# A DeltaNet inverse whose levels mask only the columns they fill, in six shared tiles per layer

## The chip, the core and the metric

One NeuronCore of a Trainium2 chip runs the whole program. The metric is the time of one execution on the device in microseconds. Engines are named as the profile names them: PE multiplies matrices (PEld is its weight load), DVE is the vector engine, ACT the scalar engine, POOL the general one, SP only issues transfers. Each engine runs its own instructions in the order in which the program lists them.

## The reference, cut to what matters

The kernel computes a two-layer backbone: three token mixers side by side (differential attention, grouped-query attention, a gated DeltaNet in both directions), merged by gates, then a feed-forward part. The change touches the DeltaNet, where each chunk needs the inverse of a unit triangular matrix:

```python
kb = kc * bc[..., None]
a_low = jnp.where(strict, jnp.einsum('bhncd,bhnsd->bhncs', kb, kc) * decay, 0.0)
eye = jnp.eye(DN_CHUNK, dtype=jnp.float32)
tmat = lax.linalg.triangular_solve(a_low + eye, jnp.broadcast_to(eye, a_low.shape),
                                   left_side=True, lower=True, unit_diagonal=True)
u = tmat @ (vc * bc[..., None])
w = tmat @ (kb * jnp.exp(gcum)[..., None])
...
def step(s, inp):
    u_i, w_i, kt_i, gl_i = inp[:4]
    v_new = u_i - jnp.einsum('bhcd,bhde->bhce', w_i, s)
    s_next = s * gl_i[..., None, None] + jnp.einsum('bhcd,bhce->bhde', kt_i, v_new)
```

## The kernel before, in words

Activations lie with features on the partitions; 512 latent and 256 context tokens make 768 columns. **Dense projections** are matmuls of a weight block `wl` with the activations `hh`, `hl` (float32 is split into a high and a low part, so each product is three matmuls) into PSUM banks `pf`; the four weight buffers are filled by a load `wr` and split by ACT and by DVE or POOL (`wunit`, L493).

**The DeltaNet** uses chunks of 128 tokens. `dn_prep` (L1435) prepares one chunk step of a pair of heads in both directions: four 128x128 matrices side by side, 512 columns, called A below. It needs one slot, the tile `pres` (its thirds hold A, its 16-bit copy and the half tile `ym`, and the decay), and one third of the shared tile `dnw` for `u16` and `t16`, the running inverse and its transpose. After a first level it runs levels 1 to 6 (L1497): PE forms `py` = A times `u16` (4 matmuls of 128 columns, 16 bit), DVE masks `py` with `lev` into `ym` (all 512 columns, though half of each matrix is only the identity), PE forms `pt` = `ym` times `t16` (4 matmuls of 128 columns) and `pu` (4 of 64 columns, the new columns alone), ACT copies `pt` into `t16` and DVE copies `pu` into the new columns of `u16` (`new_cols`, L1427). Then come two correction rounds: each is a product, a subtraction from the identity on DVE, a product and an addition on DVE, the second round in float32; POOL makes the 16-bit remainder of A before and scales the result by `beta` after (4 instructions each step). Twelve preps per layer run, two at a time. `dn_pair` (L1544) carries the state through the six steps of a head pair in sequence: product with the state, `rp` on DVE (4 instructions), product, copy on ACT, product, new state on DVE (4 instructions), and two products for the output, which DVE adds into `oacc`; it gives back four slots only at its end (`drop(4)`, L1605). It runs first for heads 0 and 1, then for heads 2 and 3.

**What sets the order.** A planner in the kernel (`Est`, L75, and `Sched`, L175) keeps an estimate of each engine's time and writes the instructions of all these chains into one program: at each point it takes a chain whose operands are estimated to be ready, by priority, and else one more matmul of the current dense job. So PE's order is fixed when the program is built, and the dense matmuls are what stands between the steps of a DeltaNet chain. The estimate of a DVE instruction grows with its columns.

**Slots.** All larger tiles come from one pool of `NSLOT` = 15 slots (L41). A chain or job that asks for slots says so first, "w" or "W" for each, and `room` (L249) grants a "W" only if `reserve` slots stay free besides:

```python
n = need.count("w") + need.count("W") + need.count("V")
spare = self.reserve if "W" in need else 1 if "V" in need else 0
return (n + spare <= self.left["w"] and all(need.count(c) <= self.left[c] for c in "tr")
        and all(need.count(c) <= len(self.est.idle[c]) for c in "mb" if c in need))
```

While the attention runs, `reserve` is 3; once only the DeltaNet is left it is 2 (L1865). The remaining DeltaNet inputs are dense jobs: `dn_inputs` (L1337) projects one head's q, k and v, asks for "tWW" before the first of the three (L1345: one tile `qk`, one tile `kv`), and the jobs stand in a line. A gate projection may stand in for a waiting job only where `reserve` is 3 (L325). The modulation products (`wm` with `cond`, `mod_late`, L572) also ask for "WW".

Of the kernel before, what the change touches and what calls it, by code (L numbers as in the profile page):

```python
# [13 lines left out]
F16 = mybir.dt.float16  # L14
BF16 = mybir.dt.bfloat16
AF = mybir.ActivationFunctionType
ALU = mybir.AluOpType
# [3 lines left out]
P = 128  # L21
# [17 lines left out]
NLEV = 7  # L39
# [339 lines left out]
def trunk(  # L379
# [5 lines left out]
    out, dbg=None,  # L385
# [3 lines left out]
    V, S, G, T = [Timed(e, k, est, tc) for e, k in ((nc.vector, "V"), (nc.scalar, "S"), (nc.gpsimd, "G"), (nc.tensor, "P"))]  # L389
# [5 lines left out]
    const = ctx.enter_context(tc.tile_pool(name="const", bufs=1))  # L395
# [31 lines left out]
    def slot(parts, n, nm, dt=F32):  # L427
        t = whole(parts, n, nm, dt)
        return [t[:, i, :] for i in range(parts)]
# [5 lines left out]
    def drop(n=1):  # L435

        sch.left["w"] += n
# [14 lines left out]
    def psml():  # L452
        return est.take("m", pools["m"].tile([P, 512], F32, tag="pm", name="pm"))

    def give(*banks):

        for t in banks:
            est.give("m", t)

    sch = Sched(est, lambda src, n: wunit(src, n))  # L460
# [10 lines left out]
    ident16 = const.tile([P, P], F16, name="ident16")  # L471
# [4 lines left out]
    nc.sync.dma_start(out=sel, in_=sel_d)  # L476
    m12 = const.tile([P, 2, 2, P], BF16, name="m12")
    nc.gpsimd.dma_start(out=m12, in_=m12_d)
    lev = const.tile([P, NLEV, 2, P], BF16, name="lev")
    nc.gpsimd.dma_start(out=lev, in_=lev_d)  # L480
    ones = const.tile([P, 1], F32, name="ones")
    V.memset(ones, 1.0)
    mhalf = const.tile([P, 24], F32, name="mhalf")
# [9 lines left out]
    def wunit(src, n):  # L493

        while sch.left["r"] < 1:
            sch.flush([g for g in sch.groups if g[4]][:1])
        sch.left["r"] -= 1
        hl = wl_.tile([P, 2, 1024], F32R, tag="wl", name="wl")
        raw = wr_.tile([P, 1024], F32, tag="wr", name="wr")
        nc.sync.dma_start(out=raw[:, 0:n], in_=src)  # L500
        lo_n[0] += 1
        eng = "G" if lo_n[0] % lo_n[1] == 0 else "V"

        def halves():
            for a, b in ((0, n // 2), (n // 2, n)):
                yield "S"
                S.copy(out=hl[:, 0, a:b], in_=raw[:, a:b])
                yield eng
                (G if eng == "G" else V).tensor_tensor(out=hl[:, 1, a:b], in0=raw[:, a:b], in1=f32(hl[:, 0, a:b]), op=ALU.subtract)
            sch.left["r"] += 1  # L510
        g = sch.defer(halves())
        g[4] = True
        return hl, g
# [9 lines left out]
    cond = const.tile([P, KC, 2 * MOD_N + 30], F32, name="cond")  # L523
# [896 lines left out]
    def v4(t):  # L1420
        return t.rearrange("p (d i c) -> p d i c", d=2, i=2)
# [5 lines left out]
    def new_cols(t, b):  # L1427


        base = t.rearrange("p (d n c) -> p d n c", d=2, c=b)  # L1430
        n = 2 * P // (2 * b)
        st = list(base.ap)
        return bass.AP(base.tensor, base.offset + b, [list(st[0]), [2 * P - b, 2], [2 * b, n], [1, b]])

    def dn_prep(l, hp, s, heads, gates, nq, work, res):  # L1435

        beta, g, gc, ngc, egc, negc, gl, kts = gates
        un = units(hp, s)
        heads = [heads[hp * 2 + i] for i in range(2)]
        a32, uc, qd = slot(3, 512, "pres")  # L1440
        if l == 0:
            for d in range(2):
                r = (FWD, BWD)[d][s] * 8 + d * 4 + hp * 2
                nc.sync.dma_start(out=a32[:, d * 256:(d + 1) * 256].rearrange("p (i c) -> p i c", i=2),
                                  in_=gr[r:r + 2].rearrange("(o i) c -> o i c", o=1).to_broadcast([P, 2, P]))
        e1 = work()
        a16, ym = [uc.bitcast(F16)[:, i * 512:(i + 1) * 512] for i in range(2)]
        u16, t16 = [e1.bitcast(F16)[:, i * 512:(i + 1) * 512] for i in range(2)]
# [33 lines left out]
        py = psml()  # L1482
        for sl, *_ in un:
            T.matmul(py[:, sl], lhsT=a16[:, sl], rhs=ident16, start=True, stop=True)
        V.tensor_tensor(out=v4(u16), in0=v4(py), in1=lev[:, 0].unsqueeze(2).to_broadcast([P, 2, 2, P]), op=ALU.mult)
        give(py)
        for d in range(2):
            V.tensor_tensor(out=v4(t16)[:, d], in0=v4(a16)[:, d], in1=lev[:, 0, 1 - d].unsqueeze(1).to_broadcast([P, 2, P]), op=ALU.mult)
        if any(t < nq for _, _, _, t, _ in un):
            yield "m"  # L1490
            pq = psml()
# [4 lines left out]
        yield "m"  # L1496
        for lv in range(1, NLEV):  # L1497
            b = 1 << lv
            py = psml()
            for sl, *_ in un:  # L1500
                T.matmul(py[:, sl], lhsT=a16[:, sl], rhs=u16[:, sl], start=True, stop=True)
            V.tensor_tensor(out=v4(ym), in0=v4(py), in1=lev[:, lv].unsqueeze(2).to_broadcast([P, 2, 2, P]), op=ALU.mult)
            give(py)
            yield "mm"
            pt = psml()
            for sl, *_ in un:
                T.matmul(pt[:, sl], lhsT=ym[:, sl], rhs=t16[:, sl], start=True, stop=True)
            pu = psml()
            for u, (sl, i, d, t, c) in enumerate(un):
                new = ym[:, sl].rearrange("p (n e c) -> p n e c", e=2, c=b)[:, :, 1 - d, :]  # L1510
                T.matmul(pu[:, u * 64:(u + 1) * 64].rearrange("p (n c) -> p n c", c=b), lhsT=t16[:, sl], rhs=new, start=True, stop=True)
            S.copy(out=t16, in_=pt)
            V.tensor_copy(out=new_cols(u16, b), in_=pu[:, 0:256].rearrange("p (d n c) -> p d n c", d=2, c=b))
            give(pt, pu)
            if lv < NLEV - 1:
                yield "m"

        G.tensor_tensor(out=ym.bitcast(BF16), in0=a32, in1=a16, op=ALU.subtract)
        for it in range(2):
            yield "m"  # L1520
            py = psml()
            for sl, *_ in un:
# [3 lines left out]
                else:  # L1526
# [3 lines left out]
                            in1=py.rearrange("p (u c) -> p u c", u=4), op=ALU.subtract)  # L1530
            give(py)
            yield "m"
            py = psml()
# [178 lines left out]
    def chunks8(nt, nm):  # L1712
        r = []
        for _ in range(4):
            r += slot(2, nt, nm)
        return r
# [18 lines left out]
    for l in range(DEPTH):  # L1735
# [3 lines left out]
        nq = nt // P  # L1739
# [51 lines left out]
        vs, res, kts, vgs, gres, hres, gates = {}, {}, [], [], {}, {}, []  # L1791
# [40 lines left out]
            sch.spawn(mod_chain(MOD_A, MOD_ROOM[0], MOD_PACE[0]), 3)  # L1832


        prep, oacc, zs, dsteps, ws0, alone = {}, {}, {}, {0: 0, 1: 0}, [], []

        def work(n):
            if not ws0:
                ws0.extend(slot(3, 512, "dnw"))
            return ws0[n % 2]  # L1840

        def preps():
            for n in range(2 * NTC):
                hp, s = divmod(n, NTC)

                def cond(n=n, hp=hp):
                    return (sum(dsteps.values()) >= n - 2 and hp * 2 + 1 in hres and hp * 2 in hres and len(gates) > 0
                            and (len(alone) > 0 or len(done) >= PREP_AT and sch.left["w"] >= PREP_LEFT))
                yield cond, dn_prep(l, hp, s, hres, gates, nq, lambda n=n: work(n), prep), "w" if n else "ww"

        def pairs():
            yield lambda: (0, 0) in prep and (len(alone) > 0 or len(done) >= PAIR_AT)
# [21 lines left out]
        i = 1 if l == 0 else 2  # L1874
        sch.spawn(mod_chain((MOD_D, MOD_F)[l], MOD_ROOM[i], MOD_PACE[i]), 3)
        sch.run()
        drop(2)
        lo_n[1] = 3
        assert sch.left == {"w": NSLOT, "t": 2, "r": 2}, sch.left
        sch.left["w"] = 1 << 30  # L1880
# [5 lines left out]
        m = chunks8(nt, "m")  # L1886
# [111 lines left out]
def _consts():  # L1998
    pos = np.arange(LAT)
    inv = (10000.0 ** (-np.arange(0, 32, 2, dtype=np.float32) / np.float32(32))).astype(np.float32)  # L2000
    ar = (pos // 64).astype(np.float32)[:, None] * inv[None]
    ac = (pos % 64).astype(np.float32)[:, None] * inv[None]
    c = np.concatenate([np.cos(ar), np.cos(ac)], 1)
    s = np.concatenate([np.sin(ar), np.sin(ac)], 1)
    rope = np.stack([np.concatenate([c, c], 1), np.concatenate([s, -s], 1)], 0)
    rope = rope.reshape(2, LAT // P, P, HD).transpose(0, 2, 1, 3)
    i = np.arange(P)
    le = (i[:, None] <= i[None, :]).astype(np.float32)
    half = (i < P // 2).astype(np.float32)[:, None]
    up = np.stack([le, le.T], 1)  # L2010
    mid = np.stack([le - half, le.T - (1 - half)], 1)
    tri = np.stack([up, mid, 1 - up], 1)
    lt = i[None, :] < i[:, None]
    strict = np.stack([lt, lt.T], 1)
    m1 = np.where(strict, -BIG, BIG)
    incl = np.stack([i[:, None] <= i[None, :], i[:, None] >= i[None, :]], 1)
    m2 = np.where(incl, BIG, -BIG)
    m12 = np.stack([m1, m2], 1).astype(np.float32)
    lev = np.zeros((P, NLEV, 2, P), np.float32)
    for n in range(NLEV):  # L2020
        b = 1 << n
        same = (i[:, None] // (2 * b)) == (i[None, :] // (2 * b))
        first = (i // b) % 2 == 0
        mk = same & first[:, None] & ~first[None, :]
        lev[:, n, 0] = np.eye(P) - mk
        lev[:, n, 1] = np.eye(P) - mk.T
    sel = np.tile(np.eye(32), (4, 1))
    return [np.ascontiguousarray(a, np.float32) for a in (rope, np.eye(P), tri, sel, m12, lev)]

# [61 lines left out]
```

## Time and profile before

| | |
|---|---|
| median of 3 runs | 2910.73 us (2908.31 to 2911.45) |
| profiled execution | 2909.93 us |
| its span, first to last instruction | 2908.2 us |
| granted TensorE clock, mean | 0.994 |
| PE busy | 2835.2 us, 97% |
| DVE busy | 1699.2 us, 58% |
| ACT busy | 1226.8 us, 42% |
| POOL busy | 811.3 us, 28% |

The profiled execution lies 0.8 us below the median; 1.7 us of it lie outside the span. The DeltaNet of the first layer lies between about 565 and 900 us of the span, that of the second between about 2090 and 2425 us. In a row of the profile, x and a number is how many instructions it stands for; line L167 is a helper that records every operation, so rows are told apart by tile names. The matmuls' ends are modelled: a burst of matmuls is shown until its last result has left the array.

### The profile page before, as it was taken

The page shows a single profiled execution, that of the slowest core. Times are in us where ns is not written, and L with a number is a line of the kernel's source. Part 1 is how long each engine was busy: PE and PEld are TensorE (multiplying, and loading weights), DVE is VectorE, ACT ScalarE, POOL GpSimd, SP SyncE. Part 2 cuts the span into 40 slices and gives each one's busy share as a digit, 9 for nine tenths or more (in the row PEclk, how much of TensorE's full clock was granted, in tenths as well). Part 3 has the DMA queues.
Part 4 walks back from the last instruction along what each step waited for, and adds up shares of the span by engine and source line. Part 5 has one row for each costly group of instructions (what it writes and reads, how often), then busy time and mean ns, then how long its engine had stood idle before and what let it go on. Part 6 is the DMA issues. An engine that isn't in the chain of part 4 may idle for free.

```text
span 2908.2 us, 48877 instructions
## 1 busy us (share of the span) xinstructions
PE 2835.2 (97%) x19304; PEld 2460.5 (85%) x19304; DVE 1699.2 (58%) x3433; ACT 1226.8 (42%) x2522; POOL 811.3 (28%) x832
## 2 busy tenths in 40 slices
PE   7999999999999999999999999999999999999999
PEld 5888898888788888888888889898878788888888
DVE  4555767868766545333334456577787866553343
ACT  4444556645443224222222345466654443343332
POOL 3414231123322432112112242441123333422221
PEclk9999999999999999999999999999999999999999
DMA  8242211241312631121212321212131316323332
GB/s 312 90 147 77 68 49 55 62 157 59 113 57 97 221 109 59 51 73 53 72 58 68 97 75 55 61 59 62 57 122 44 132 66 203 127 85 107 97 98 87
DMA packets 100117, 271.99 MB, mean 94 GB/s; under 512 B 14209, under 2 KB 26417, under 8 KB 99889
## 3 DMA queue, kind: packets, MB, share of 16 engines
q1 hardware_dynamic: 88800, 247.31, 26.5%
q10 hardware_dynamic: 10800, 20.98, 1.8%
q8 instruction: 152, 2.49, 0.4%
q0 software_dynamic: 288, 0.59, 0.1%
q14 instruction: 77, 0.62, 0.1%
HBM read 240.56 MB, written 28.86 MB: 93 GB/s over the span
## 4 chain that ended last, share of the span: by engine, by line
PE 56%; DVE 3%; POOL 2%; issue 1%; ACT 1%; DMA 1%; SPq 0%; POOLq 0%; ACTq 0%; DVEq 0%
PE pf L167 46%; PE pm L167 7%; PE pb L167 2%; DVE wl L167 0%; POOL wl L167 0%; POOL m L167 0%; POOL pres L167 0%; DVE mx L167 0%; DMA th<-gd 0%; DVE dnw L167 0%; DVE oacc L167 0%; DVE pres L167 0%; POOL rn L167 0%; POOL rtmp L167 0%; DVE p L167 0%
## 5 line engine op out<-in xcount | busy, mean ns | idle before, releaser
L167 PE MATMUL pf<-hh,wl 128*128 128x512 f32 (+1 forms) x4192 | 1022.6, 359 | 9.9 <-ACT hh L167 6.2
L167 PEld LDWEIGHTS pf<-hh,wl 128*128 128x128 f32 x4192 | 698.1, 190 | 105.0 <-ACT hh L167 9.2
L167 POOL TENSOR_TENSOR wl<-wr,wl 128x512 fp32r<-128x512 f32 (+3 forms) x258 | 326.0, 1280 | 940.0 <-ACT wl L167 934.1
L167 PE MATMUL pf<-hl,wl 128*128 128x512 f32 (+1 forms) x2096 | 575.7, 359 | 0.9 <-POOL hl L167 0.6
L167 ACT CAST wl<-wr 128x512 fp32r<-128x512 f32 (+3 forms) x620 | 341.2, 588 | 491.0 <-PE pf L167 423.4
L167 PEld LDWEIGHTS pf<-hl,wl 128*128 128x128 f32 x2096 | 361.0, 190 | 47.6 <-POOL hl L167 1.8
L167 PE MATMUL pf<-wl,hh 128*128 128x256 f32 (+2 forms) x1664 | 321.7, 288 | 0.0
L167 PE MATMUL pf<-g,wl 128*128 128x512 f32 (+1 forms) x1629 | 307.3, 350 | 0.0
L167 PEld LDWEIGHTS pf<-g,wl 128*128 128x128 f32 x1629 | 263.8, 189 | 42.3 <-ACT g L167 1.9
L167 DVE TENSOR_TENSOR wl<-wr,wl 128x512 fp32r<-128x512 f32 (+4 forms) x362 | 263.3, 751 | 51.5 <-ACT wl L167 49.7
L167 PEld LDWEIGHTS pf<-wl,hh 128*128 128x128 f32 x1664 | 264.5, 192 | 5.9 <-issue 4.1
L167 PE MATMUL pf<-wl,hl 128*128 128x256 f32 (+2 forms) x832 | 241.1, 290 | 0.0
L167 DVE SCALAR_TENSOR_TENSOR x<-pf,gate,x 128x512 f32<-128x512 f32 (+1 forms) x126 | 80.4, 640 | 243.6 <-PE pf L167 237.0
L167 PE MATMUL pm<-dnw,pres 128*128 128x128 f16 (+1 forms) x1824 | 195.3, 236 | 6.2 <-POOL pres L167 3.0
L167 DVE SCALAR_TENSOR_TENSOR ff<-pf,cf,ff 128x511 f32<-128x511 f32 (+1 forms) x132 | 86.9, 658 | 184.5 <-ACT ff L167 183.2
L167 ACT ACTIVATE p<-pb,nb,r 128x768 f32<-128x768 f32 (+1 forms) x160 | 145.1, 908 | 104.5 <-DVE nb L167 82.7
L167 PE MATMUL pf<-ohl,wl 128*128 128x512 f32 (+1 forms) x864 | 171.6, 359 | 1.5 <-DVE ohl L167 0.7
L167 PEld LDWEIGHTS pf<-ohl,wl 128*128 128x128 f32 x864 | 143.9, 191 | 26.4 <-DVE ohl L167 1.8
L167 PEld LDWEIGHTS pf<-wl,hl 128*128 128x128 f32 x832 | 160.1, 192 | 2.7 <-issue 2.5
L167 DVE TENSOR_REDUCE mx<-pb 128x1 f32<-128x768 f32 (+1 forms) x160 | 133.5, 845 | 41.1 <-PE pb L167 39.9
L167 ACT CAST dnw<-pm 128x512 f16<-128x512 f32 x144 | 83.9, 585 | 143.8 <-PE pm L167 140.3
L167 PEld LDWEIGHTS <-pres 128*128 128x128 f16 (+1 forms) x1440 | 87.3, 98 | 58.2 <-issue 32.3
(246 smaller groups left out, 4083.9 us busy)
## 6 DMA issues: line engine op xcount, KB each, us to landing
wm<-in_w_mod_dram SPq DMA_DIRECT2D x96, 512.0 KB, 5.4
wr<-in_w_dram SPq DMA_DIRECT2D x88, 512.0 KB, 3.6
wr<-in_w_f_dram SPq DMA_DIRECT2D x80, 512.0 KB, 3.6
wr<-in_w_t_dram SPq DMA_DIRECT2D x32, 512.0 KB, 3.7
wr<-in_w_br_dram SPq DMA_DIRECT2D x24, 512.0 KB, 3.6
wr<-in_w_dram SPq DMA_DIRECT2D x32, 384.0 KB, 3.1
wr<-in_w_dram SPq DMA_DIRECT2D x32, 320.0 KB, 2.9
gd<-th ACTq DMA_DIRECT2D x24, 384.0 KB, 2.3
```

Source lines behind the costliest of these rows:

```text
L167: ins = f(*args, **kw)
```

## The change

A level masks only the 256 columns that it fills. The product `ym` moves out of the prep's own slot into six tiles, one per level, that all preps of a layer share: one slot `dny`, taken by the first prep. POOL writes the identity into each of the six once per layer; a level then writes its new columns over it and nothing else. So that two preps don't use one level's tile at once, a prep asks before each level whether its tile is in use. The first prep of a layer asks for three slots in place of two, and the layer gives back three at the end. The masks `lev` are laid out anew on the host; their size in memory is the same.

```diff
-    def dn_prep(l, hp, s, heads, gates, nq, work, res):
+    def dn_prep(l, hp, s, heads, gates, nq, work, yms, res):
...
         for lv in range(1, NLEV):
             b = 1 << lv
+            yield lambda lv=lv: lv not in yms()[-1] and sch.room("m")
+            yms()[-1].add(lv)
             py = psml()
             for sl, *_ in un:
                 T.matmul(py[:, sl], lhsT=a16[:, sl], rhs=u16[:, sl], start=True, stop=True)
-            V.tensor_tensor(out=v4(ym), in0=v4(py), in1=lev[:, lv].unsqueeze(2).to_broadcast([P, 2, 2, P]), op=ALU.mult)
+
+            yl = yms()[lv - 1]
+            V.tensor_tensor(out=new_cols(yl, b), in0=new_cols(py, b), in1=levn[lv].rearrange("p (d n c) -> p d n c", d=2, c=b), op=ALU.mult)
             give(py)
             yield "mm"
             pt = psml()
             for sl, *_ in un:
-                T.matmul(pt[:, sl], lhsT=ym[:, sl], rhs=t16[:, sl], start=True, stop=True)
+                T.matmul(pt[:, sl], lhsT=yl[:, sl], rhs=t16[:, sl], start=True, stop=True)
             pu = psml()
             for u, (sl, i, d, t, c) in enumerate(un):
-                new = ym[:, sl].rearrange("p (n e c) -> p n e c", e=2, c=b)[:, :, 1 - d, :]
+                new = yl[:, sl].rearrange("p (n e c) -> p n e c", e=2, c=b)[:, :, 1 - d, :]
                 T.matmul(pu[:, u * 64:(u + 1) * 64].rearrange("p (n c) -> p n c", c=b), lhsT=t16[:, sl], rhs=new, start=True, stop=True)
+            yms()[-1].remove(lv)
...
+        def yms():
+            if not ys:
+                t = whole(3, 512, "dny").bitcast(F16)
+                ys.extend(t[:, i // 2, i % 2 * 512:(i % 2 + 1) * 512] for i in range(NLEV - 1))
+                ys.append(set())
+                for y in ys[:NLEV - 1]:
+                    G.tensor_copy(out=y.rearrange("p (u c) -> p u c", u=4), in_=ident16.unsqueeze(1).to_broadcast([P, 4, P]))
+            return ys
...
-                yield cond, dn_prep(l, hp, s, hres, gates, nq, lambda n=n: work(n), prep), "w" if n else "ww"
+                yield cond, dn_prep(l, hp, s, hres, gates, nq, lambda n=n: work(n), yms, prep), "w" if n else "www"
...
-        drop(2)
+        drop(3)
```

The change moves instructions on every engine, since the planner's estimate of a mask falls with its columns and one slot less is free. Three places follow. In them `pf` are dense matmuls, `wm` modulation products; a product of a level reads `pres` (A, and before the change `ym`) or `dny` (the new tiles) and `dnw`; LDWEIGHTS is the weight load of the 16-bit matmul behind it; each such pair stands four times.

PE, first layer, levels of the fifth and sixth prep, the last two of heads 0 and 1, before:

```order
L167 MATMUL pm<-dnw,pres 128x128
L167 LDWEIGHTS dnw
L167 MATMUL pm<-pres,dnw 128x64
...
L167 MATMUL pf<-hh,wl 128x256 x2
L167 MATMUL pf<-hl,wl 128x256 x2
L167 MATMUL pf<-hh,wl 128x256 x2
...
L167 MATMUL pm<-identr,kv 128x128 x4
```

In the program before, dense matmuls or transposes of the next head's inputs stand between the products of one level and the next; the longest piece of PE's order in the two DeltaNet stages without a dense or modulation matmul has 59 rows.

PE, first layer, the same preps and the step of `dn_pair` behind them, with the change:

```order
L167 MATMUL pf<-hh,wl 128x512
L167 LDWEIGHTS pres
L167 MATMUL pm<-dnw,pres 128x128
...
L167 LDWEIGHTS dny
L167 MATMUL pm<-dnw,dny 128x128
...
L167 MATMUL pm<-dny,dnw 128x64
...
L167 MATMUL pm<-dnw,qk 128x128 x4
L167 MATMUL pm<-dnw,pres 128x128
L167 MATMUL pm<-wm,cond 32x256
```

Between that `pf` row and that `wm` row stand 286 rows, all of the DeltaNet: the last four levels of two preps in step and half of one before, both preps' corrections, and one and a half steps of `dn_pair`. In the second layer there is one such piece of 260 rows; no other piece of either stage has more than 58.

POOL, first layer, the first prep, with the change:

```order
L167 TENSOR_TENSOR wl<-wr,wl 128x512 x2
L167 TENSOR_TENSOR pres<-pres 128x512
L167 COPY dny<-ident_88 128x512 x6
L167 TENSOR_TENSOR wl<-wr,wl 128x512 x4
L167 TENSOR_SCALAR pres<-pres,beta 128x128 x8
```

The six copies are new; they stand behind two remainders of A and ahead of the low halves of four weight blocks' pieces.

## Rows read from the trace of the kernel before

**Rows 1.** The page, part 1: busy us (share of the span), instructions.

```profile
PE 2835.2 (97%) x19304; PEld 2460.5 (85%) x19304; DVE 1699.2 (58%) x3433; ACT 1226.8 (42%) x2522; POOL 811.3 (28%) x832
```

**Rows 2.** Both DeltaNet stages: length, busy PE, PEld, DVE, ACT, POOL, clock, DMA share, GB/s.

```profile
560.00:945.00 385.00, 379.00 (x3300) 325.20 (x3299) 282.57 (x636) 177.77 (x398) 113.30 (x114) 1.00 0.29 97
2080.00:2430.00 350.00, 342.50 (x2933) 280.13 (x2932) 265.19 (x594) 167.90 (x365) 111.64 (x118) 1.00 0.28 93
```

**Rows 3.** PE's waits, first layer's stage, 560 to 945 us: total, times, longest.

```profile
PE pm L167 <- DVE pres L167: 2.0, 3, 1.6
PE pm L167 <- POOL pres L167: 1.3, 3, 0.7
...
PE pm L167 <- DVE dnw L167: 0.7, 3, 0.3
```

**Rows 4.** PE's waits, second layer's stage, 2080 to 2480 us.

```profile
PE pm L167 <- DVE oacc L167: 2.7, 2, 1.8
PE pm L167 <- DVE dnw L167: 2.1, 3, 1.8
PE pm L167 <- POOL pres L167: 1.9, 2, 1.2
```

**Rows 5.** DVE's groups by shape: busy us, mean ns | idle before, releaser.

```profile
L167 DVE TENSOR_TENSOR pres<-pm,lev 128x512 f16<-128x512 f32 x144 | 97.4, 686 | 31.3 <-PE pm L167 29.8
...
L167 DVE CAST dnw<-pm 128x256 f16<-128x256 f32 x144 | 59.9, 420 | 28.1 <-PE pm L167 27.0
...
L167 DVE SCALAR_TENSOR_TENSOR dnw<-pm,negc,kv 128x128 f32<-128x128 f32 x80 | 22.5, 342 | 6.8 <-PE pm L167 6.7
...
L167 DVE TENSOR_TENSOR otmp<-pm,otmp 64x256 f32<-64x256 f32 x40 | 16.8, 420 | 12.7 <-ACT otmp L167 12.0
...
L167 DVE TENSOR_TENSOR pres<-identr,pm 128x512 bf16<-128x512 f32 x24 | 16.3, 682 | 10.0 <-PE pm L167 10.0
...
L167 DVE TENSOR_TENSOR oacc<-pm,oacc 128x128 f32<-128x128 f32 x40 | 9.7, 281 | 6.9 <-PE pm L167 6.8
```

**Rows 6.** ACT's and POOL's groups by shape.

```profile
L167 ACT CAST dnw<-pm 128x512 f16<-128x512 f32 x144 | 83.9, 585 | 143.8 <-PE pm L167 140.3 <-DVE gate L167 1.2 <-ACT kv L167 0.2
...
L167 POOL TENSOR_TENSOR wl<-wr,wl 128x512 fp32r<-128x512 f32 x214 | 284.5, 1345 | 794.8 <-ACT wl L167 788.9 <-DVE pres L167 5.8
L167 POOL TENSOR_SCALAR pres<-pres,beta 128x128 f32<-128x128 f32 x96 | 62.2, 666 | 102.8 <-DVE pres L167 95.5 <-DVE modF L167 7.3
...
L167 POOL TENSOR_TENSOR pres<-pres 128x512 bf16<-128x512 f32 x24 | 28.6, 1195 | 75.7 <-PE pm L167 70.1 <-DVE pres L167 5.5
```

**Rows 7.** Timeline, first layer, one level of two preps: start us, us, engine, operation.

```profile
603.43 0.40 PE L167 MATMUL pm<-dnw,pres 128*128 128x128 f16 x4
...
603.66 0.28 PE L167 MATMUL pm<-pres,dnw 128*128 128x64 f16 x4
...
603.78 0.39 PE L167 MATMUL pm<-dnw,pres 128*128 128x128 f16 x4
...
603.98 0.77 DVE L167 CAST dnw<-pm 128x256 f16<-128x256 f32 x2 [0.93 <-PE pm L167]
...
604.46 0.38 PE L167 MATMUL pm<-dnw,pres 128*128 128x128 f16 x4
...
604.88 1.29 DVE L167 TENSOR_TENSOR pres<-pm,lev 128x512 f16<-128x512 f32 x2
...
605.73 0.40 PE L167 MATMUL pm<-dnw,pres 128*128 128x128 f16 x4
```

**Rows 8.** Timeline near 706.85 us: four float32 products of the DeltaNet (eight matmuls).

```profile
706.85 1.06 PE L167 MATMUL pm<-dnw,pres 128*128 128x128 f32 x8
```

**Rows 9.** Stretches at the end of the second stage, columns as in rows 2.

```profile
2423.00:2427.00 4.00, 2.19 (x11) 1.36 (x10) 3.19 (x5) 0.93 (x2) 4.00 (x4) 1.00 0.01 4
2427.00:2431.00 4.00, 3.10 (x10) 2.62 (x11) 2.50 (x4) 0.00 (x0) 0.30 (x1) 0.50 0.61 197
2431.00:2435.00 4.00, 4.00 (x13) 3.18 (x12) 0.45 (x1) 0.00 (x0) 0.00 (x0) 0.64 1.00 322
```

More of the change, by code (lines that the diff above doesn't have):

```diff
@@ L478, in trunk @@
     nc.gpsimd.dma_start(out=m12, in_=m12_d)
-    lev = const.tile([P, NLEV, 2, P], BF16, name="lev")
+    lev = const.tile([P, 2 * NLEV, P], BF16, name="lev")
     nc.gpsimd.dma_start(out=lev, in_=lev_d)
+    lev0, levn = lev[:, 0:2], [lev[:, 2 * n:2 * n + 2].rearrange("p a c -> p (a c)") for n in range(NLEV)]
     ones = const.tile([P, 1], F32, name="ones")
@@ L1484, in dn_prep @@
             T.matmul(py[:, sl], lhsT=a16[:, sl], rhs=ident16, start=True, stop=True)
-        V.tensor_tensor(out=v4(u16), in0=v4(py), in1=lev[:, 0].unsqueeze(2).to_broadcast([P, 2, 2, P]), op=ALU.mult)
+        V.tensor_tensor(out=v4(u16), in0=v4(py), in1=lev0.unsqueeze(2).to_broadcast([P, 2, 2, P]), op=ALU.mult)
         give(py)
         for d in range(2):
-            V.tensor_tensor(out=v4(t16)[:, d], in0=v4(a16)[:, d], in1=lev[:, 0, 1 - d].unsqueeze(1).to_broadcast([P, 2, P]), op=ALU.mult)
+            V.tensor_tensor(out=v4(t16)[:, d], in0=v4(a16)[:, d], in1=lev0[:, 1 - d].unsqueeze(1).to_broadcast([P, 2, P]), op=ALU.mult)
         if any(t < nq for _, _, _, t, _ in un):
@@ L1832, in trunk @@
             sch.spawn(mod_chain(MOD_A, MOD_ROOM[0], MOD_PACE[0]), 3)
-        prep, oacc, zs, dsteps, ws0, alone = {}, {}, {}, {0: 0, 1: 0}, [], []
+        prep, oacc, zs, dsteps, ws0, alone, ys = {}, {}, {}, {0: 0, 1: 0}, [], [], []
         def work(n):
@@ L2024, in _consts @@
         mk = same & first[:, None] & ~first[None, :]
-        lev[:, n, 0] = np.eye(P) - mk
-        lev[:, n, 1] = np.eye(P) - mk.T
+        for d, m in enumerate((mk, mk.T)):
+            if n == 0:
+                lev[:, n, d] = np.eye(P) - m
+            else:
+                new = ~first if d == 0 else first
+                lev[:, n, d] = np.concatenate([(np.eye(P) - m)[:, new]] * 2, 1)
+    lev = lev.reshape(P, 2 * NLEV, P)
     sel = np.tile(np.eye(32), (4, 1))
```

## The prediction

> **What bounds the kernel now.** I read the page's busy times first, then the two DeltaNet stages as stretches, then PE's waits inside them. PE is busy for 97% of the span [rows 1]; no other engine comes near. The time is therefore PE's work plus PE's idle time, and a step on DVE counts only where PE waits for it. In the two stages, 385 and 350 us long, PE is idle for 6.0 and 7.5 us [rows 2]. The waits that belong to the DeltaNet's preparation are 2.0, 1.3 and 0.7 us in the first [rows 3] and 2.1 and 1.9 us in the second, where another 2.7 us are the tail of its output, `oacc` [rows 4]. So the chain of a prep, long as it is, is covered almost everywhere by dense matmuls that the planner puts between its steps. All that a shorter mask can win is these 8.0 us; everything else depends on the cover staying.
>
> **What the change removes.** 144 masks of 512 columns at 686 ns become masks of 256. DVE's product out of PSUM with 256 float32 results takes 420 ns, and its copy into the same strided columns also takes 420, so strides cost nothing there [rows 5]. I take 0.42 us: 0.27 us less per mask, 38 us of DVE in all. DVE is busy for 58% [rows 1], so this is worth nothing by itself. Per prep the chain gets six times 0.27 us shorter. POOL's remainder of A, 1.195 us [rows 6], no longer has to wait until the last level has read `ym`; it can be done earlier. Both take from the 8.0 us of waits; those on masks and on POOL are about half of them, so I take 4 us back, between 0 and 8.
>
> **What it adds.** PE's work is the same, matmul for matmul. POOL writes 512 columns of identity twelve times. The trace has no such copy: two-source work of that width takes 1.345 us, a one-source 128 columns 0.666 us [rows 6], so 0.6 to 1.4 us each, 4 to 8 us in a row per layer. POOL is busy for 28% [rows 1]. Behind them on POOL stand the low halves of weights and the scaling of the first preps; the planner splits weight blocks up to four ahead of their use, and PE would have to run through those first, so I cost the copies at nothing. If that cover were gone the whole row would be paid, up to 8 us per layer. The first level needs only the first copy. The wait for a tile in use is nothing either: the planner holds the second prep back until PE's two products are written down, and PE runs them in order anyway.
>
> **The slot is what costs.** After the attention, slots are held by `qk` and `kv` of three heads (6), `dnw` (2), `oacc` (1) and two or three `pres`: 11 or 12 of 15. Head 3's inputs ask for two with two in reserve, so they need 4 free. Before, there are 4 whenever only two `pres` live. With `dny` there are 3 at most, so the job stands until `dn_pair` of heads 0 and 1 ends and gives four back. The dense line stands behind it, no gate projection may take its place with a reserve of 2, and the modulation products ask for the same four. PE's order shows the outcome: one piece of 286 rows in the first layer and one of 260 in the second hold nothing but DeltaNet, where 59 was the most before.
>
> What do these pieces cost? First the levels. Two preps go in step. By the timeline [rows 7] four products of 128 columns take 0.23 us of PE before the next burst starts, four of 64 take 0.12, so PE's work for one level of both is 2 x (0.23 + 0.12 + 0.23) = 1.16 us. The chain of one prep is: `pt` 0.23, `pu` until its last result 0.28, to DVE 0.04, copy 0.42, back to PE 0.09, `py` 0.38, to DVE 0.04, mask 0.42, back 0.17: 2.07 us (it was 2.34). The second prep's DVE steps fit between, since DVE has 4 x 0.42 = 1.68 us. So each level without dense work leaves PE 0.91 us idle. The first layer has four such levels and one half covered: 4.1 us. The second has three: 2.7 us.
>
> Then the corrections and the state. Four float32 products take about 1.0 us [rows 8], 16-bit ones 0.40 with their drain [rows 7]. The first prep's corrections are 0.62 (eight matmuls) + 0.68 + 0.40 + 0.68 + 1.06 + 0.68 + 0.40 + 0.68 and 0.67 of hand-overs (four of 0.04, three of 0.17): 5.9 us. The second prep, one level and part of a correction behind on the same DVE, ends at about 10.0 us. In the first layer DVE then makes `rp` (4 x 0.342 [rows 5]); the product with it starts at 10.5 and ends at 11.9; ACT copies for 0.585 [rows 6]; the state's product starts at 12.7, its four DVE steps end at 14.6; the output's sums, 4 x (0.281 + 0.342), at 17.1; the next `rp` lets the next product start at about 18 us. PE's own work up to there is ten 16-bit bursts, one of 64 columns, and eight float32 products: 10 x 0.23 + 0.12 + 8 x 0.97 = 10.2 us. PE loses about 8 us. In the second layer the second prep lies a level further behind and fills some of the gaps; the same count gives 6 us up to the next `wm`, and 1 us when the second prep's result is scaled on POOL after it: 7 us.
>
> Bounds: if the estimate's order is loose and DVE or ACT still work off a dense job there, each piece loses up to 4 us more; if the two preps and the state run fully side by side, the second part loses half, 4 and 3.5 us.
>
> **The clock.** In 2423 to 2427 us PE was busy for 2.19 of 4 us, and for the next 8 us the granted clock was 0.50 and 0.64, half of 2.4 GHz for most of it [rows 9]: 3.4 us of full clock lost. The new pieces are thin too, 1.16 us of work in 2.07. I take one fall per layer, half of it hidden since PE waits there anyway: 2 x 1.7 = 3.4 us; bounds 0 and two whole falls per layer, 13.6. The Trainium skill ("TensorE: Matmul & The Clock Gate", Part 1) says that the low clock is the default state and that activity releases it. By that rule the falls would last as long as the thin pieces do. The trace agrees that it returns once PE is full again: 1.00 from 2435 us on.
>
> **Sum.** 4.1 + 8 + 2.7 + 7 - 4 + 3.4 = 21.2 us on the profiled execution's 2909.93 us, which lies 0.8 us below the median: **2931 us**, 0.7% slower. A measurement of this kernel can tell about 0.2%, 5.8 us, from no change.
>
> **Rivals.**
> 1. *The shorter chain wins* (faster). If the pieces' idle time is only moved, because preps that run ahead let later stages, the `oacc` tail with its 2.7 us and its clock fall among them, run without waits, 8.0 + 2.7 + 3.4 = 14.1 us come back; with 7 us left as the price of both pieces that is 2903 us. It decides if the two pieces together lose less than 14.1 us. For it: in the first layer the change has 10 us of gate projections behind the last DeltaNet product. Against: PE's total work is fixed, and an idle microsecond in a piece isn't given back by fuller stretches elsewhere. Chance 0.07.
> 2. *The pieces are thin, but cost little*: half the loss of the second parts, no clock fall, 8 us regained: 21.8 / 2 - 8 = 3 us, 2913 us. For it: chains on four engines overlap better than my hand count. Chance 0.13.
> 3. *The clock stays low through the pieces* and what follows: 13.6 in place of 3.4, 2941 us. For it: rows 9. The page named above would have it so for as long as PE stays thin. Chance 0.2.
> 4. *The change doesn't do what it says*: the strided mask takes as long as before (0.68 us), levels then take 2.34 us, and 7 more levels' 0.27 us are lost: 2933 us. Inside the range; chance 0.03, and 0.57 for the forecast itself.
>
> **How the numbers follow.** Forecast, rival 3 and rival 4 are slower by over 0.2%, as is a small part of rival 2: 0.83. Faster is rival 1 with some of its span within the bound: 0.06. The rest, 0.11, is no difference. The range leaves out rival 1 and the lower half of rival 2 below, and the worst of rival 3 above: 2913 to 2945 us.
>
> **What would show it.** Right: masks of 256 columns at 0.42 us; two stretches of about 25 us, around 690 and 2240 us of the span, with PE idle for 10 to 13 us each, waiting for DVE and POOL on `dny`, `pres` and `dnw`, and no `pf` in them; a clock of 0.5 in or right behind them. Wrong: PE's waits in the two stages together below 13 us, or a new wait on POOL's copies at the first prep. If the stretches are there but cost 5 us each, the hand-overs are what I mis-sized; if they cost 20, it is the clock.

## The result, and the profile after

With the change the kernel takes 2927.53 us (median of 4 runs, 2925.80 to 2929.83) beside 2909.95 us for the kernel before (4 runs, 2908.31 to 2911.45): ratio 1.0057, 95% interval 1.0045 to 1.0069. It is slower by 17.6 us, three times the 5.8 us that a measurement tells from no change; the forecast was 21.2 us slower. The profiled execution took 2926.18 us, 16.25 more than that of before.

The page of the changed kernel, part 1 (columns as in [rows 1]):

```profile
PE 2838.1 (97%) x19304; PEld 2465.7 (84%) x19304; DVE 1676.0 (57%) x3433; ACT 1225.2 (42%) x2522; POOL 817.3 (28%) x844
```

Beside [rows 1] PE's work is the same, matmul for matmul, though its busy time reads 2.9 us more; DVE has 23.2 us less to do, POOL 12 instructions and 6.0 us more. So at least 13 of the 16 us are idle time of PE. Where it lies shows in both DeltaNet stages, the changed kernel first, then the kernel before over the same stretches (columns as in [rows 2]):

```profile
560.00:955.00 395.00, 381.57 (x3301) 325.34 (x3301) 273.57 (x644) 176.70 (x398) 116.24 (x121) 1.00 0.28 95
2090.00:2450.00 360.00, 346.71 (x2951) 287.75 (x2951) 257.10 (x597) 168.49 (x366) 115.35 (x124) 1.00 0.28 93
```

```profile
560.00:955.00 395.00, 389.00 (x3359) 333.86 (x3358) 289.91 (x648) 179.02 (x400) 113.30 (x114) 1.00 0.30 100
2090.00:2450.00 360.00, 352.50 (x2946) 287.42 (x2945) 268.60 (x599) 166.97 (x364) 112.17 (x119) 0.99 0.31 103
```

PE is idle for 13.4 and 13.3 us where it was idle for 6.0 and 7.5. The second figure of a row understates the loss, since the modelled ends of short bursts count as busy. PE's waits in the changed kernel, first layer (560 to 955 us), then second (2090 to 2490 us), as in [rows 3, 4]:

```profile
PE pm L167 <- DVE dnw L167: 4.2, 6, 1.5
PE pm L167 <- DVE pres L167: 2.1, 5, 0.8
PE pm L167 <- DVE dny L167: 2.0, 3, 1.2
...
PE pm L167 <- DVE dnw L167: 6.5, 9, 1.7
PE pm L167 <- DVE oacc L167: 1.5, 1, 1.5
PE pm L167 <- DVE dny L167: 1.3, 3, 0.6
```

The waits on POOL's `pres`, 1.3 and 1.9 us before, are gone; those on `dnw`, 0.7 and 2.1 us, have grown to 4.2 and 6.5. The new time lies in one place per layer. PE in the first layer, from the last dense matmul before the piece to the first product of the modulation behind it:

```profile
712.79 0.47 PE L167 MATMUL pf<-hh,wl 128*128 128x512 f32 x1
...
715.44 0.40 PE L167 MATMUL pm<-dnw,dny 128*128 128x128 f16 x4
...
717.37 0.40 PE L167 MATMUL pm<-dnw,dny 128*128 128x128 f16 x4
...
719.30 0.40 PE L167 MATMUL pm<-dnw,dny 128*128 128x128 f16 x4
...
720.33 0.91 PE L167 MATMUL pm<-dnw,pres 128*128 128x128 f16 x12
721.79 0.38 PE L167 MATMUL pm<-pres,dnw 128*128 128x128 bf16 x4 [0.55 <-DVE pres L167]
...
726.69 1.16 PE L167 MATMUL pm<-pres 128*128 128x128 f32 x8 [0.82 <-DVE pres L167]
728.63 0.38 PE L167 MATMUL pm<-dnw 128*128 128x128 bf16 x4 [0.78 <-DVE dnw L167]
...
732.40 1.16 PE L167 MATMUL pm<-dnw,pres 128*128 128x128 f32 x8 [0.68 <-ACT dnw L167]
...
737.71 0.46 PE L167 MATMUL pm<-dnw,pres 128*128 128x128 f32 x2 [1.47 <-DVE dnw L167]
738.10 0.62 PE L167 MATMUL pm<-wm,cond 128*32 128x256 f32 x2
```

From 713 to 738 us there is no `pf`. A level comes every 1.93 us, of which PE works 1.16; then the products of the corrections and of the state wait nine times for the step of DVE or ACT ahead of them. The second layer has the same picture from 2225 to 2245 us.

How far that explains the whole is read from places that both programs pass: PE's groups by tile, with the first and last start (the group of `dnw` and `pres` once for each layer, the first layer's on top). The changed kernel:

```profile
L167 PE MATMUL pf<-mhl,wl x648: 277/283/640, 1050.1 to 2554.2; 128*128 128x256 f32 x84, 128*128 128x512 f32 x78
...
L167 PE MATMUL pf<-ohl,wl x864: 277/389/478, 948.3 to 2503.9; 128*128 128x512 f32 x115, 128*128 128x256 f32 x58
...
L167 PE MATMUL pm<-dnw,pres x640: 216/219/377, 597.5 to 934.4; 128*128 128x128 f16 x96, 128*128 128x128 f32 x64
...
L167 PE MATMUL pm<-dnw,pres x608: 216/219/377, 2124.3 to 2430.3; 128*128 128x128 f16 x94, 128*128 128x128 f32 x58
```

The kernel before:

```profile
L167 PE MATMUL pf<-mhl,wl x648: 277/283/470, 1038.0 to 2538.1; 128*128 128x256 f32 x84, 128*128 128x512 f32 x78
...
L167 PE MATMUL pf<-ohl,wl x864: 274/389/776, 930.4 to 2489.2; 128*128 128x512 f32 x116, 128*128 128x256 f32 x57
...
L167 PE MATMUL pm<-dnw,pres x928: 216/219/377, 595.2 to 934.3; 128*128 128x128 f16 x135, 128*128 128x128 f32 x51
...
L167 PE MATMUL pm<-dnw,pres x896: 216/219/377, 2112.9 to 2417.9; 128*128 128x128 f16 x134, 128*128 128x128 f32 x46
```

The first `mhl`, behind the first layer's DeltaNet, is 12.1 us later (1050.1 against 1038.0); 2.3 of them are there by the first product of that group (597.5 against 595.2), behind a fall of the clock at 112 us, 1.7 us of full clock, that the old profile doesn't have. That fall isn't the change's: the kernel with an unused slot and one in reserve (below), whose PE has the order of the kernel before, has one at 113 us. So the first stage costs 9.8 us. The first `dnw` of the second layer is 11.4 us late, the last `ohl`, behind its DeltaNet, 14.7: the second stage adds 3.3 us. Behind it 1.4 us more are lost by the last `mhl`, with another fall at 2508 us, 1.7 us of full clock again. The kernel before has its fall inside the second stage, after 2427 us, 3.4 us [rows 9]. Over the whole execution the falls weigh the same, the mean granted clock is 0.994 in both; with the falls left out the stages cost 9.8 and up to 6.7 us, which makes up the 16.25 between the two profiled executions.

### The profile page after: what moved, and what is told of

It reads as the page before. It is cut to its first block, busy times and chain, and to the rows that moved or that the text cites. A ratio compares the mean times of both kernels' runs of the same rounds, so it can differ in the third digit from the quotient of the medians.

```text
span 2924.2 us, 48911 instructions
## 1 busy us (share of the span) xinstructions
PE 2838.1 (97%) x19304; PEld 2465.7 (84%) x19304; DVE 1676.0 (57%) x3433; ACT 1225.2 (42%) x2522; POOL 817.3 (28%) x844
## 3 DMA queue, kind: packets, MB, share of 16 engines
q8 instruction: 152, 2.49, 0.4%
## 5 line engine op out<-in xcount | busy, mean ns | idle before, releaser
L167 PE MATMUL pm<-dnw,pres 128*128 128x128 f16 (+1 forms) x1248 | 144.1, 243 | 8.8 <-DVE dnw L167 6.3
L167 POOL TENSOR_TENSOR g<-ff,g 128x768 fp32r<-128x768 f32 (+1 forms) x44 | 69.8, 1585 | 233.7 <-ACT g L167 233.7
```

Of the source, the lines that this page charges most:

```text
L167: ins = f(*args, **kw)
```

## The experiments

**The theory.** The tile `dny` holds a fifteenth part of the slots, so that a dense job asking for two slots with two in reserve is refused, the dense line stops, and PE runs a chain bare. The rivals: the planner's smaller estimate of a mask moves the dense work (nothing to do with slots); the POOL copies or the tiles in common are what PE waits for; the strided mask isn't faster. Ratios stand against the kernel before on the same chip: 2910.36 us for the first four kernels, 2911.12 us on another chip for the last four (the one request, the unused slot with one in reserve, the doubled mask, the remainder on DVE).

**The slot alone.** The kernel before, masks as before, with a slot taken by the first prep, filled and used for nothing:

```diff
             b = 1 << lv
+            hold()
             py = psml()
...
+        def hold():
+            if not held:
+                held.append(whole(3, 512, "dny"))
+                G.memset(held[0], 0.0)
...
-                yield cond, dn_prep(l, hp, s, hres, gates, nq, lambda n=n: work(n), prep), "w" if n else "ww"
+                yield cond, dn_prep(l, hp, s, hres, gates, nq, lambda n=n: work(n), hold, prep), "w" if n else "www"
...
-        drop(2)
+        drop(3)
```

> The kernel before, with one slot per layer taken at the first prep's first level, filled once by POOL and never used; masks stay 512 columns wide, and the planner knows them as such. Its PE order has one piece of 395 rows without a dense or modulation matmul in the first layer and one of 349 in the second. Theory 'the slot': slower than before by what these pieces cost, about 15 us (six levels at 2.34 - 1.16 us of PE idle, 8 us behind) in the first layer and 11 in the second: 2928 to 2942 us, with PE's waits on dnw and pres up in two stretches of 25 to 35 us. Rival 'the planner's new estimate of the masks made the pieces': 2907 to 2914 us. Rival 'POOL's six copies': 2909 to 2914 us, since one fill stands in for six.

Measured: 2936.08 us (2934.23 to 2939.76), ratio 1.0090, interval 1.0076 to 1.0104. A slot that nobody uses costs 26 us, more than the whole change. Its waits of PE in the first stage:

```profile
PE pm L167 <- DVE pres L167: 5.7, 11, 1.4
PE pm L167 <- DVE dnw L167: 4.0, 8, 1.5
```

They are of the kind that the change has, with the wide mask (`pres`) on top. The narrow masks, then, don't cause the loss; with the slot taken, the change as a whole is faster than the slot alone, by 8.5 us (2927.53 against 2936.08; the ratios are 1.0057 and 1.0090). Part of that is the clock, which in this kernel falls within the pieces (below).

**The change with one slot in reserve.**

```diff
-        sch.limit, sch.reserve = lambda: 3 * KC, 2
+        sch.limit, sch.reserve = lambda: 3 * KC, 1
```

> The changed kernel with a reserve of 1 in place of 2 once only the DeltaNet is left, so that head 3's inputs need 3 free slots. Everything of the change stays: narrow masks, six tiles, POOL's copies. No piece without dense work is longer than 43 rows. Theory 'the slot': the loss goes, and what the shorter chain is worth is left: 2902 to 2912 us. Rival 'the planner's estimate' or 'POOL's copies' or 'the shared tiles': 2922 to 2932 us, as the change.

Measured: 2908.55 us, ratio 0.9995 (0.9986 to 1.0004). The copies, the tiles in common and the narrow masks are all kept, and the loss is gone; the longest piece of PE's order without dense work has 43 rows. Both stages (columns as in [rows 2]):

```profile
560.00:955.00 395.00, 387.29 (x3359) 333.22 (x3358) 274.43 (x651) 177.97 (x402) 117.43 (x121) 1.00 0.31 101
2090.00:2450.00 360.00, 353.54 (x2967) 291.85 (x2967) 258.87 (x604) 169.24 (x367) 119.06 (x127) 1.00 0.31 107
```

PE is idle for 7.7 and 6.5 us, in all 14.2, against 13.5 in the kernel before over the same stretches. So the copies, the sharing and the shorter chain, taken together, neither cost nor bring anything that shows.

**The planner's estimate, from both sides.** First the kernel before, its planner told that a mask has 256 columns; then the changed kernel, its planner told that it has 512.

```diff
+        if e == "V" and op == "tensor_tensor" and out.tensor.name.startswith("pres") and any(i.tensor.name.startswith("lev") for i in ins):
+            n = 256
```

> The kernel before; the planner alone is told that a level's mask has 256 columns, DVE still does 512. No slot is taken. No piece is longer than 41 rows. Theory 'the slot': the same as before within 0.2%, or up to 5 us slower where PE now comes too early for a mask: 2908 to 2916 us. Rival 'the planner's new estimate': 2922 to 2932 us.

Measured: 2912.40 us, ratio 1.0003 (0.9994 to 1.0011).

```diff
+        if e == "V" and op == "tensor_tensor" and out.tensor.name.startswith("dny"):
+            n = 512
```

> The changed kernel; the planner alone is told that a mask still has 512 columns, DVE does 256. The pieces are there, 286 and 252 rows. Theory 'the slot': as the change, 2922 to 2932 us. Rival 'the planner's new estimate': back to 2906 to 2914 us.

Measured: 2924.99 us, ratio 1.0052 (1.0038 to 1.0066), with pieces of 286 and 252 rows. The loss stays with the slot and doesn't come with the estimate: this rival falls.

**Which demand stops the line.** The changed kernel, reserve 2 as it was; only the inputs of heads 2 and 3 may go down to one free slot:

```diff
-                yield "tWW" if i == 0 else "t"
+                yield ("tWW" if h < 2 else "tVV") if i == 0 else "t"
```

> The changed kernel with the reserve still 2, but the inputs of heads 2 and 3 alone may go ahead with one slot in reserve; modulation products and gate projections ask as before. No piece of PE's order without dense work is longer than 44 rows. Theory 'head 3's inputs, held up for want of a slot, stop the dense line': the whole loss goes, 2904 to 2913 us. Rival 'the modulation products, which ask for the same slots, are what is missing': 2918 to 2930 us.

Measured: 2914.01 us (2907.91 to 2920.47), ratio 1.0008 (0.9999 to 1.0018), a miss by 1 us, just above what was expected; the longest piece has 44 rows. By the ratios (1.0008 here, 1.0057 with the change) some 14 of 17 us are back with this one line, and the interval holds the kernel before. Which of the two heads' requests it is was not told apart. In the second stage a wait for a weight load is new:

```profile
PE pm L167 <- DMA wm<-in_w_mod_dram: 2.3, 1, 2.3
```

The modulation products still ask for four free slots here; that their load now comes late is what the row shows, why it does was not tried.

**The slot alone, with one in reserve.** The first experiment again, reserve 1:

> The kernel before with one slot held per layer and a reserve of 1: PE's order is that of the kernel before again (longest pieces 59 and 58 rows), masks are wide. Theory 'the slot, by way of the reserve': the loss of the held slot goes entirely, 2907 to 2914 us. Rival 'the slot costs in some other way, by memory or by the fill': 2920 us or more.

Measured: 2911.02 us (2907.47 to 2914.51), ratio 0.9995 (0.9986 to 1.0004). PE's order is that of the kernel before, row for row. So the slot costs only by way of the reserve. Beside the second experiment this is also a comparison of the wide masks with the narrow ones and the copies and shared tiles that come with them, slot and reserve alike: 0.9995 in both, each against the kernel before on its own chip (2911.02 and 2908.55 us on two chips). The shorter mask, so made, can't be told from nothing.

**Every mask twice.** Reserve 1, and each level's mask is done two times by DVE, the second over the first:

```diff
             V.tensor_tensor(out=new_cols(yl, b), in0=new_cols(py, b), in1=levn[lv].rearrange("p (d n c) -> p d n c", d=2, c=b), op=ALU.mult)
+            V.tensor_tensor(out=new_cols(yl, b), in0=new_cols(py, b), in1=levn[lv].rearrange("p (d n c) -> p d n c", d=2, c=b), op=ALU.mult)
```

> The changed kernel with a reserve of 1, and every level's mask done twice on DVE: 144 more masks of 0.42 us, so that a level takes DVE 0.16 us longer than before the change. The planner counts both. Theory 'a mask lies under dense matmuls': 2906 to 2917 us, within 0.3% of the kernel with one mask, though DVE works 60 us more. Rival 'the width of the mask is on the path': 72 steps of two preps at 0.42 us, up to 30 us slower, 2930 us or more.

Measured: 2919.42 us (2912.72 to 2921.64), ratio 1.0024 (1.0014 to 1.0033): a miss, above the end of what was expected: 0.29% above the second experiment by the two ratios, 8 us (11 by the times, on two chips). The group and the waits of PE on it in the first and second stage:

```profile
L167 DVE TENSOR_TENSOR dny<-pm,lev 128x256 f16<-128x256 f32 x288 | 115.6, 419 | 22.8 <-PE pm L167 19.6
...
PE pm L167 <- DVE dny L167: 5.5, 5, 2.9
...
PE pm L167 <- DVE dny L167: 2.6, 3, 1.1
```

PE is idle for 22.0 us in the two stages, where it was 14.2 in the second experiment. These waits are not all of it: a single one of 4.5 us on `oacc` stands in the first stage too. DVE's 62 us more (1730.6 busy against 1668.4) make 8 to 11 us: the cover holds for most of a longer chain, not for all of it. It doesn't follow that a shorter chain wins in the same measure; the pair above shows none of it.

**POOL's remainder on DVE.** Why did DVE save 23 us only, where 38 were worked out? In the changed kernel the first level's masks, which the change doesn't touch, went from 366 to 610 ns (the kernel before, then the changed one):

```profile
L167 DVE TENSOR_TENSOR dnw<-pres,lev 128x256 f16<-128x256 f16 x48 | 16.0, 366 | 1.9 <-ACT pres L167 1.7
```

```profile
L167 DVE TENSOR_TENSOR dnw<-pres,lev 128x256 f16<-128x256 f16 x48 | 27.8, 610 | 1.7 <-ACT pres L167 1.4
```

The suspect is POOL's remainder of A, which no longer waits for PE (its idle time is now ended by ACT, in [rows 6] by PE) and runs beside those masks. Reserve 1, with

```diff
-        G.tensor_tensor(out=ym.bitcast(BF16), in0=a32, in1=a16, op=ALU.subtract)
+        V.tensor_tensor(out=ym.bitcast(BF16), in0=a32, in1=a16, op=ALU.subtract)
```

> The changed kernel with a reserve of 1, and the 16-bit remainder of A made by DVE in place of POOL. Reading behind it: DVE's first-level masks of 256 columns out of SBUF in 16 bit, 0.37 us on the mean before and 0.61 with the change, are slowed by POOL's remainder, which no longer waits for the last level and now runs beside them. If so their mean falls to 0.28 to 0.35 us. If the new masks or the planner's order slow them, it stays at 0.5 or more. The time, by every theory here: 2905 to 2916 us.

Measured: 2910.83 us, ratio 0.9992 (0.9983 to 1.0002). The masks in this kernel, which took 499 ns in the second experiment:

```profile
L167 DVE TENSOR_TENSOR dnw<-pres,lev 128x256 f16<-128x256 f16 x48 | 17.2, 390 | 0.8 <-ACT pres L167 0.7
```

390 ns is a miss, a little above the 0.28 to 0.35 us expected, and about what the kernel before has. The starts and ends in the traces say why: in this kernel 33 of the 48 masks lie beside no work of POOL and take 0.28 us on average, the other 15 lie beside POOL's other work, low halves of weights above all, and take 0.63. In the changed kernel 17 lie alone (0.28), 20 beside a remainder (0.81) and 11 beside POOL's other work (0.75); in the kernel before none lies beside a remainder. So the remainder makes the rise, and POOL's other work does the same where it meets them; the time of the kernel doesn't move by it.

No version tried beats the kernel before by more than the 0.2% that can be told.

## Why the prediction was right, point by point

**The mechanism held.** The loss is the slot: alone it costs 26 us, with one slot less in reserve nothing; the demand that stops the line is that of the inputs of heads 2 and 3, as the run that eases it alone shows. The two pieces lie near where they were put (713 to 738 and 2225 to 2245 us, forecast around 690 and 2240). That the two preps go in step and PE waits for DVE there is in the rows. Two of the signs that were named did not come: a clock of 0.5 in or behind the pieces, and 10 to 13 us of idle time in each; they have 10.3 and 8.0, as worked out next.

**The levels** were slightly too dear: a period of 1.93 us in place of 2.07, so 0.77 us idle per level in place of 0.91. Four levels make 3.1 us in place of the 4.1 taken for four and a half, three make 2.3 in place of 2.7. The mask took 421 ns, as worked out:

```profile
L167 DVE TENSOR_TENSOR dny<-pm,lev 128x256 f16<-128x256 f32 x144 | 59.7, 421 | 29.6 <-PE pm L167 26.6
L167 POOL COPY dny<-ident 128x512 f16<-128x512 f16 x12 | 7.5, 669 | 0.0
```

**Corrections and state**: in the first layer they last 17.2 us, from 720.56 (the burst at 720.33 starts with 0.23 us of the last level) to 737.71. The rows hold 64 float32 matmuls (eight times 0.97), nine 16-bit bursts of 0.23 and one of 0.12: 10.0 us of work, so 7.2 us lost for the 8 forecast. In the second they last from 2230.43 to 2245.74 us:

```profile
2230.20 0.83 PE L167 MATMUL pm<-dnw,pres 128*128 128x128 f16 x12
...
2245.74 1.07 PE L167 MATMUL pm<-wm,cond 128*32 128x256 f32 x16
```

The same count with one burst of 0.12 more gives 10.1 of 15.3 us, 5.2 lost, and a wait of 0.5 behind: 5.7 us for the 7 forecast. For the first layer 3.1 + 7.2 is 10.3 us, where the places that both programs pass gave 9.8.

**The clock was the term that was mis-sized.** I took 3.4 us for a fall per layer. There is none in either piece. The thinnest stretches of the first (columns as in [rows 9]):

```profile
724.00:728.00 4.00, 2.48 (x25) 1.89 (x24) 2.60 (x5) 1.54 (x6) 1.79 (x4) 1.00 0.00 0
728.00:732.00 4.00, 2.56 (x20) 2.21 (x19) 2.39 (x6) 0.79 (x3) 2.64 (x5) 1.00 0.00 0
```

The first experiment, with longer pieces of the same kind and wide masks, does have falls, as rival 3 had it:

```profile
724.00:728.00 4.00, 2.86 (x44) 2.16 (x41) 2.68 (x7) 2.12 (x4) 1.15 (x1) 1.00 0.00 0
728.00:732.00 4.00, 3.07 (x25) 2.65 (x23) 2.31 (x5) 1.81 (x5) 1.15 (x1) 0.75 0.00 0
732.00:736.00 4.00, 2.82 (x24) 2.22 (x22) 2.52 (x4) 0.95 (x3) 1.67 (x3) 0.83 0.01 4
736.00:740.00 4.00, 2.71 (x13) 2.45 (x13) 2.21 (x6) 0.68 (x3) 2.45 (x6) 0.60 0.00 0
740.00:744.00 4.00, 3.33 (x15) 3.03 (x15) 0.30 (x2) 0.58 (x1) 0.56 (x1) 0.50 0.00 0
```

Each slice's 4 us times what its clock lacks, these and the others from 712 to 748 us lose 8.5 us of full clock and those of the second piece 3.4; the two profiled executions lie 13.6 us apart (2939.76 and 2926.18). Not all of the lost clock need be time, since PE waits in the pieces anyway, so the price of rival 3 was of the right order; it was paid in this kernel and not in the changed one. PE's busy time ahead of the falls doesn't tell the two kernels apart: in the first experiment it was 2.86 of 4 us ahead of the fall at 730 us, and the changed kernel kept its clock behind 2.48 and 2.56. So did the changed kernel whose planner was told 512 columns, behind 2.49 from 724 to 728 us. Why one falls and the other doesn't stays open.

The Trainium skill ("TensorE: Matmul & The Clock Gate", Part 1) was cited ahead for the low clock as the default state, which activity releases. As it was read there, the low clock would last as long as PE is thin; the 25 us from 713 us on, at 1.00 throughout, don't show that.

**The regained 4 us** were not there to be had. The waits on POOL's remainder did go, 3.2 us of [rows 3, 4]; but where nothing else disturbs (the second experiment) PE's idle time in both stages is 14.2 us against 13.5. Others came: ACT's `dnw` with 1.9 us, and `th` of DVE with 2.3 us in the second stage. As I read it, PE comes earlier by a wait that goes to the next place where it must wait; no run tries that by itself.

**Where a piece of rival 1 came true**: the second stage costs 3.3 us and not the 8.0 that its piece costs (2.3 + 5.7). Up to 6.5 us are there to make up the 4.7 between them: `oacc` waits for 1.5 us in place of 2.7, POOL's 1.9 are gone, and the fall of the clock of [rows 9], 3.4 us, isn't there. Once the fall is taken off, 1.3 of the 4.7 us are left for the other two. And the fall can't be put down to the change. The kernel with the unused slot and one in reserve, whose PE has the order of the kernel before, waits 2.7 us on `oacc` as that does, keeps its clock there, and has a fall at 2492 us instead:

```profile
2423.00:2427.00 4.00, 2.81 (x13) 1.99 (x11) 2.74 (x9) 1.14 (x2) 3.46 (x4) 1.00 0.10 39
2427.00:2431.00 4.00, 2.49 (x14) 2.05 (x15) 3.74 (x5) 0.00 (x0) 1.54 (x1) 1.00 0.29 85
...
2492.00:2496.00 4.00, 3.93 (x10) 3.12 (x11) 1.98 (x4) 1.66 (x3) 1.82 (x2) 0.57 0.96 367
```

So 2931 against 2927.5 us: the levels 1.4 us too dear, corrections and state 2.1, the clock 3.4, and 4 us credited that didn't come in the way it was thought: 21.2 - 1.4 - 2.1 - 3.4 + 4 = 18.3, for 17.6 measured between the medians and 16.25 between the profiled executions, which the rows are from. That is, the sign and the size rest on the two pieces, 18.3 us together by the rows where 21.8 were forecast. That the forecast came within 4 us is in part luck: a credit of 4 us that wasn't there and a price of 3.4 us for falls that didn't come nearly cancel. What stays open is how the rest is shared between the tail and the regained waits; falls of the clock at other places in different executions are as large as what is left. One sum of the prediction doesn't fit its words: rival 2 speaks of half the loss of the second parts and halves both pieces whole (21.8 / 2); with the levels kept it is 6.8 + 7.5 - 8, some 6 us.

## What to carry to other kernels

Before a buffer is taken for good, find who asks for the last free ones and with what reserve: here 23 us less of vector work won nothing and one slot of 15 cost 17 us, because the refused request was the dense work that covered a chain of dependent steps. Read the order of the instructions on the bounding engine for stretches without its independent work; the loss is the period of the chain less the engine's own work, step by step. Shortening a chain that was covered won nothing here that could be told, and a longer one, by some 60 us of DVE, still cost a part.

## What the hardware showed that had not been expected

**A DVE product with both inputs in SBUF slows down beside POOL's work there.** The 16-bit masks of the first level, in the changed kernel, once beside POOL's remainder and once started while POOL was idle:

```profile
645.22 1.16 POOL L167 TENSOR_TENSOR pres<-pres 128x512 bf16<-128x512 f32 x1
645.45 1.09 DVE L167 TENSOR_TENSOR dnw<-pres,lev 128x256 f16<-128x256 f16 x1
...
646.85 0.28 DVE L167 TENSOR_TENSOR dnw<-pres,lev 128x256 f16<-128x256 f16 x1
```

The same instruction takes 1.09 us beside it, ending 0.16 us behind POOL's, and 0.28 started alone; 0.28 is also the mean of the 17 that meet no work of POOL. Over the 48 of them this makes 27.8 us where it was 16.0, so 11.8 of the 38 us that the shorter masks saved on DVE. The Trainium skill ("GPSIMD Engine Reference", section 1, Specifications) says that POOL shares its SBUF interfaces with the vector engine and that DVE instructions with two inputs from SBUF contend with it. The run with the remainder on DVE agrees: 390 ns in place of 499. The level masks, whose first input comes from PSUM, kept their 421 ns; the 36 of 144 that lie beside work of POOL take 419 on average.

**A one-source 16-bit copy on POOL** of 128x512 took 0.67 us on average, at the lower bound of the 0.6 to 1.4 us that had been set.

**The clock's falls come at different places in kernels with the same order of PE.** The kernel before falls after 2427 us and not near 112; the kernel with the unused slot and one in reserve falls at 113 and 2492 us and not near 2427 (one profiled execution of each). So a fall of 1.7 or 3.4 us at one place should not be read as the work of a change.
